# One of seven block products of a Strassen-type output projection is built from seven smaller ones

## The chip, the cores and the metric

The kernel runs on one core of one Trainium2 chip. The metric is the time of one execution on the device in microseconds (us). The profile is one execution, recorded by the hardware profiler: its times count from the first instruction, and its engines are called PE (TensorE, matrix products), PEld (its weight loads), DVE (VectorE), ACT (ScalarE), POOL (GpSimd) and SP (SyncE, which here only issues transfers).

## What is computed

One layer of a transformer trunk on 512 tokens of width 2048, all in 32-bit floats: a normalisation, attention over a sliding window of 128 tokens with 32 query heads, an output projection, a gated embedding, and a last normalisation.

```python
def reference(x, p, ...):
    hn = rmsnorm(x, norm_g)
    x = x + swa_mixer(hn, ...)              # ends with (out * silu(gate)) @ w_out
    emb = p @ ple_proj
    g = sigmoid(rmsnorm(x, ple_norm) @ ple_gate)
    x = x + emb * g
    return rmsnorm(x, final_g)
```

The change is within `(out * silu(gate)) @ w_out`: a 512 x 2048 matrix (the gated attention output, transposed in `gates`) times a 2048 x 2048 weight matrix, added to `x`.

## The kernel before

**Precision.** TensorE multiplies rounded 32-bit numbers (`F32R`). To keep the full precision, every operand is split into a high part (a cast on ACT) and a low part (the difference, on DVE), and `mm3` (lines 123 to 128) makes each product of three matmuls: high by high, high by low, low by high. A matmul takes a 128 x 128 stationary block and 128 x 512 moving columns.

**Stages.** First keys, values and the first queries; then a long stage in which attention runs beside the rest of the input projections (64 blocks of work in a loop, line 828); then the output projection (lines 967 to 1000); then the gate of the embedding with `ple_gate`, built the same way as the output projection (lines 1101 on); then the last rows. TensorE's and SP's instructions keep the order of the program. From line 870 to the second product of the gate, DVE, ACT and POOL are ordered by a planner, which puts an operation where it reckons the engine free and its inputs there.

**Seven products instead of eight.** For the output projection both matrices are cut into 2 x 2 blocks: the gated output into a11, a12, a21, a22 (1024 rows of the contraction or 256 tokens each way), the weights into four blocks of 1024 x 1024. Seven block products of sums of blocks give the result. They are numbered, and run in the order

```python
ORDER_OUT, ORDER_PLE = (1, 7, 2, 6, 5, 3, 4), (2, 7, 1, 6, 5, 3, 4)
```

Each product runs as two units (p, jj), one for each half of the block's 1024 columns (`unit`, line 903). A unit has four pieces m = 0 to 3. A piece is 128 x 1024 numbers of weights (512 KB): two chunks of 128 rows by 512 columns. With two blocks of 128 tokens, two chunks and three passes a piece gives 12 matmuls, a unit 48, a product 96. Products 6, 5 and 3 go on summing in the PSUM banks in which product 1 left its result (`chain`); the others take fresh banks. After a unit, `add_y` (line 950) adds or subtracts its two 128 x 512 results to `x1`, on DVE, from a list `later` of which some are put out after each piece. Results of product 1 are held back (`held`, `waiting`) until their place in `x1` has been loaded. When a 128 x 512 tile of `x1` is complete, `squares` sums its squares on ACT.

**Weight sums.** Products 7, 5 and 6 need sums of two weight blocks. They are made in DRAM while attention runs: `sum_weights` (line 640) copies one block to a scratch tile (issued on SP) and some steps later adds the other onto it by an adding transfer (issued on POOL), a step or two after each of the 64 blocks. `SUM_STEPS` counts them. Products 1, 2 and 3 take plain blocks of `w_out`. Product 4's piece is not loaded by itself: product 6's pieces lie in eight buffers of their own (`grown`, kind "seed"), and once a piece has been split, POOL adds product 4's block onto it there (kind "grow").

**Pieces.** The class `Pieces` (line 647) is the queue for the weight pieces. `get(i)` first looks ahead: it issues loads up to piece i + 3 (i + 4 in the gate stage, which has a fourth buffer, `fourth`), seeds up to i + 6, and splits pieces up to i + 2. A load waits until the piece that had its buffer has been split. There are three buffers for high parts and three for low parts (`whi`, `wlo`), so the cast of piece i + 3 waits until TensorE has finished piece i.

**Forms.** The token side is prepared by `Forms.steps` (line 755): for each product a sum of blocks on DVE where it needs one (in place, in `gates`), then high and low parts, in eight buffers, one product ahead.

Of the kernel before, what the change touches and what calls it, by code (L numbers as in the profile page):

```python
# [55 lines left out]
def trunk_kernel(ctx: ExitStack, tc: tile.TileContext, a: dict):  # L56
# [558 lines left out]

    def blk(t):
        return slice(t * P, (t + 1) * P)
# [3 lines left out]
    ORDER_OUT, ORDER_PLE = (1, 7, 2, 6, 5, 3, 4), (2, 7, 1, 6, 5, 3, 4)  # L621
# [9 lines left out]
    for nm, p in SUMS:  # L631
# [15 lines left out]
    class Pieces:  # L647
# [9 lines left out]
        def _prepare(self, i):  # L657
# [35 lines left out]
        def ahead(self, i):  # L693

            last = len(self.specs) - 9
            for n in range(max(i, 0), min(i + 6, last) + 1):
                kind = self.specs[n][0]
                if n not in self.base and n >= self.done and kind != "grow" and (kind == "seed" or n <= i + (4 if i >= at_ple[ORDER_PLE[0], 0] else 3)):
# [19 lines left out]
    def add_stage(nm, order):  # L718
# [7 lines left out]
        for p in order:  # L726
            for jj in range(2):
# [4 lines left out]
                at[p, jj] = len(B.specs)  # L732
                for m in range(4):
                    if (nm, p) in SUMS:
# [5 lines left out]
                    B.add(kind, src, (nm, jj, m) if p in growing else None)  # L740
                if p != 4:
# [4 lines left out]
    at_ple = add_stage("ple_gate", ORDER_PLE)  # L746

    class Forms:
# [154 lines left out]
    def unit(p, jj, at, forms, todo):  # L903
# [4 lines left out]
        for m in range(4):  # L908
            bh, bl = B.get(at[p, jj] + m)
# [6 lines left out]
            todo()  # L916
        return ps
# [31 lines left out]

    def add_y(p, jj, tb, ps):  # L950
        c11, c12, c21, c22 = ((2 * v + jj, 2 * u + tb) for u in range(2) for v in range(2))
        whither = {
            1: [(c11, -1)], 2: [(c11, 1)], 7: [(c22, 1), (c21, -1)], 6: [(c21, -1)], 5: [(c22, 1)], 3: [(c12, 1)],
            4: [(c21, 1)],
        }[p]
        for (j, t), sign in whither:
            xt = x1[j][:, t, :]
            if sign > 0:
                nc.vector.tensor_add(xt, ps, xt)
            else:  # L960
                nc.vector.tensor_sub(xt, xt, ps)
            if p in (2, 5, 3, 4):
                squares(t, j)
# [4 lines left out]
    waiting = {(7, 0): (1, 0), (2, 0): (1, 1)}  # L968
    held = {}
    for n, p in enumerate(ORDER_OUT):  # L970
        nxt = out_forms.steps(ORDER_OUT[n + 1]) if n < 6 else iter(())
        for jj in range(2):
            later.extend(held.pop(waiting.get((p, jj)), ()))
            calls = iter(range(4))

# [12 lines left out]
            ps = unit(p, jj, at_out, out_forms, todo)  # L988
# [99 lines left out]
    spare = late.tile([P, 2 * WE], F32R, name="spare")  # L1088
# [12 lines left out]
    for n, p in enumerate(ORDER_PLE[:-1]):  # L1101
# [8 lines left out]
        for jj in range(2):  # L1110
# [18 lines left out]
            if p in (1, 5, 3):  # L1129
                w = B.get(at_ple[p, jj] + 4)  # L1130
# [14 lines left out]
    def block(jj, tb, tag, e_tag, c=slice(0, 512)):  # L1145

        ps = bank(f"last{jj}_{tb}_{c.start}", tag)
        for k in range(8):
            fh, fl = f[k // 2]
            bh, bl = B.made[at_ple[4, jj] + k // 2]  # L1150
# [155 lines left out]
```

## Time and profile before

| | us |
|---|---|
| median of 3 runs | 797.12 |
| lowest and highest | 797.02, 797.53 |
| profiled execution, whole | 797.26 |
| its span, first to last instruction | 795.3 |

The mean granted clock of TensorE in the profiled execution was 0.996 of full speed. The span shares and the views of the trace stand in the prediction. To read them: a row of the timeline has the start, the duration, the engine, the line of the kernel and what is written from what, and in square brackets how long the engine stood idle before it and what ended that. A row of the stage view has, for each engine, busy microseconds and the count of instructions, then TensorE's granted clock, the busy share of the 16 DMA engines (overlapping records can bring it a little over 1) and GB/s. In the DMA view, `q1 hardware_dynamic` are the transfers that SP issues and `q0 software_dynamic` those that POOL issues, with packets, MB and the share of 16 engines; an issue's row ends with the microseconds until it has landed. A matmul's end is modelled: matmuls overlap, so their spacing and not their duration says what they take.

### The profile page before, as it was taken

How to read it: one execution, taken by the hardware profiler on the slowest of the kernel's cores; microseconds unless marked ns; L12 is line 12 of the kernel's file. 1: busy time of each engine (PE TensorE's matmuls, PEld its weight loads, DVE VectorE, ACT ScalarE, POOL GpSimd, SP SyncE). 2: the span in 40 equal slices, each digit the busy share in tenths (PEclk: the TensorE clock that was granted, in tenths of full speed). 3: DMA queues.
4: the chain of work that ended last, by engine and by line, in shares of the span. 5: the costliest groups of instructions: out<-in, count | busy, mean ns of one | idle time of the engine just before them, and what ended most of it. 6: DMA issues, size and time to landing. Idle time of an engine off the chain costs nothing.

```text
span 795.3 us, 10980 instructions
## 1 busy us (share of the span) xinstructions
PE 785.0 (99%) x3758; PEld 657.6 (83%) x3758; DVE 587.3 (74%) x1026; ACT 500.6 (63%) x1057; POOL 116.2 (15%) x238
## 2 busy tenths in 40 slices
PE   9999999999999999999999999999999999999995
PEld 8888888888888888888888888888888888888885
DVE  4547697877878597777768898766646757988896
ACT  6643576666767576666757655555568656656765
POOL 0021213131212213121212100030000020200000
PEclk9999999999999999999999999999999999999998
DMA  9983489697869968787875479997603996787633
GB/s 348 271 218 110 117 259 242 172 254 183 226 168 255 206 198 230 192 238 158 247 170 146 119 264 328 352 261 239 205 30 132 373 211 194 159 227 218 180 106 106
DMA packets 42919, 165.28 MB, mean 208 GB/s; under 512 B 6048, under 2 KB 7072, under 8 KB 39024
## 3 DMA queue, kind: packets, MB, share of 16 engines
q1 hardware_dynamic: 35456, 129.67, 48.5%
q0 software_dynamic: 7408, 34.93, 23.9%
q8 instruction: 29, 0.48, 0.2%
q14 instruction: 26, 0.21, 0.1%
HBM read 157.70 MB, written 46.19 MB: 256 GB/s over the span
## 4 chain that ended last, share of the span: by engine, by line
PE 98%; DMA 0%; DVE 0%; ACT 0%; issue 0%; ACTq 0%; DVEq 0%
PE gps L126 7%; PE gps L128 7%; PE gps L127 7%; PE qps L126 7%; PE qps L128 7%; PE qps L127 7%; PE o L126 6%; PE o L128 6%; PE o L127 6%; PE g L126 5%; PE g L127 5%; PE g L128 5%; PE s L462 2%; PE o L557 2%; PE vps L279 2%; PE pt L515 2%
## 5 line engine op out<-in xcount | busy, mean ns | idle before, releaser
L680 DVE TENSOR_TENSOR blo<-braw,bhi 128x1024 fp32r<-128x1024 f32 x80 | 97.8, 1222 | 39.7 <-ACT bhi L679 39.5
L679 ACT CAST bhi<-braw 128x1024 fp32r<-128x1024 f32 x80 | 84.2, 1052 | 65.6 <-PE o L128 19.8
L126 PE MATMUL gps<-xh,whi 128*128 128x512 f32 x256 | 99.9, 390 | 0.1
L128 PE MATMUL gps<-xh,wlo 128*128 128x512 f32 x256 | 99.9, 390 | 0.0
L127 PE MATMUL gps<-xl,whi 128*128 128x512 f32 x256 | 99.8, 390 | 0.0
L126 PE MATMUL o<-bhi,fho 128*128 128x512 f32 x224 | 87.7, 392 | 0.0
L126 PE MATMUL qps<-xh,whi 128*128 128x512 f32 x224 | 87.7, 391 | 0.0
L128 PE MATMUL qps<-xh,wlo 128*128 128x512 f32 x224 | 87.4, 390 | 0.0
L127 PE MATMUL qps<-xl,whi 128*128 128x512 f32 x224 | 87.3, 390 | 0.0
L128 PE MATMUL o<-bhi,flo 128*128 128x512 f32 x224 | 87.2, 389 | 0.0
L127 PE MATMUL o<-blo,fho 128*128 128x512 f32 x224 | 87.2, 389 | 0.0
L110 DVE TENSOR_TENSOR wlo<-wraw,whi 128x1024 fp32r<-128x1024 f32 x60 | 73.8, 1231 | 2.7 <-ACT whi L109 2.4
L126 PE MATMUL g<-bhi,fhg 128*128 128x512 f32 x192 | 75.1, 391 | 0.0
L128 PE MATMUL g<-bhi,flg 128*128 128x512 f32 x192 | 74.8, 389 | 0.0
L127 PE MATMUL g<-blo,fhg 128*128 128x512 f32 x192 | 74.7, 389 | 0.0
L531 POOL TENSOR_SCALAR_AFFINE_SELECT own<-r 64x512 fp32r<-64x512 f32 (+1 forms) x48 | 32.5, 677 | 255.8 <-DVE r L521 255.8
L520 ACT CAST r<-pt 128x256 fp32r<-128x256 f32 x64 | 23.8, 371 | 71.5 <-PE pt L515 71.1
L521 DVE TENSOR_TENSOR r<-pt,r 128x256 fp32r<-128x256 f32 x64 | 27.1, 424 | 55.5 <-ACT r L520 54.8
L109 ACT CAST whi<-wraw 128x1024 fp32r<-128x1024 f32 x60 | 62.4, 1041 | 5.3 <-issue 3.9
L680 DVE TENSOR_TENSOR blo<-grown,bhi 128x1024 fp32r<-128x1024 f32 x32 | 39.1, 1224 | 23.5 <-ACT bhi L679 23.4
L128 PEld LDWEIGHTS gps<-xh,wlo 128*128 128x128 f32 x256 | 48.0, 188 | 10.1
L126 PEld LDWEIGHTS gps<-xh,whi 128*128 128x128 f32 x256 | 48.1, 188 | 9.4 <-PE vps L279 0.5
(207 smaller groups left out, 1736.5 us busy)
## 6 DMA issues: line engine op xcount, KB each, us to landing
wraw<-in_w_gate_in SPq DMA_DIRECT2D x32, 512.0 KB, 5.7
wraw<-in_w_q SPq DMA_DIRECT2D x28, 512.0 KB, 5.0
w_out<-in_w_out POOLq DMA_DIRECT2D x24, 512.0 KB, 7.1
braw<-in_w_out SPq DMA_DIRECT2D x24, 512.0 KB, 4.0
braw<-in_ple_gate SPq DMA_DIRECT2D x24, 512.0 KB, 4.2
xw<-in_first SPq DMA_DIRECT2D x14, 640.5 KB, 6.5
w_out<-in_w_out SPq DMA_DIRECT2D x16, 512.0 KB, 5.8
ple_gate<-in_ple_gate SPq DMA_DIRECT2D x16, 512.0 KB, 6.6
```

Source lines behind the costliest of these rows:

```text
L109: nc.scalar.copy(hi, raw)
L110: nc.vector.tensor_sub(lo, raw, hi.bitcast(F32))
L126: nc.tensor.matmul(ps, sh, mh, start=first, stop=False, skip_group_check=more)
L127: nc.tensor.matmul(ps, sh, ml, start=False, stop=False, skip_group_check=more)
L128: nc.tensor.matmul(ps, sl, mh, start=False, stop=last, skip_group_check=more)
L279: nc.tensor.matmul(v_ps[t], h[:, c], both[:, :, 256:512], start=f, stop=e, skip_group_check=True)
L462: nc.tensor.matmul(s_ps[:, u, : 2 * n], st, key[:, :, first : first + n], start=True, stop=True)
L520: nc.scalar.copy(rh, src)
L521: nc.vector.tensor_sub(rl, src, rh.bitcast(F32))
L531: nc.gpsimd.affine_select(out=flat(own), in_=flat(r).bitcast(F32), pattern=[[0, 8], [sign, HB]], compare_op=ALU.is_ge, fill=0.0, base=-HB ...
L679: nc.scalar.copy(hi, raw)
L680: nc.vector.tensor_sub(lo, raw, hi.bitcast(F32))
```

## The change

Product 2 (a12 by one plain weight block of 1024 x 1024, added to the first quadrant of the result) is no longer run as a product of its own. Its two factors and its result are cut into 2 x 2 blocks again, 512 rows of the contraction by 128 tokens and 512 x 512 weights, and seven small products by the same scheme give it. A small product has two pieces of 128 x 1024 weights, each for one block of 128 tokens: 6 matmuls a piece. The pieces of the small products are placed behind pieces of the large ones (`SMALL`): two small pieces in each of the units (6,0), (6,1) and (3,0), four in (5,0) and (5,1).

What goes with it: small products 7, 5, 6 and 4 take sums of weights, two tiles each, which `sum_weights` makes beside the others (48 copies and 48 adding transfers instead of 40, in the same 64 blocks). Small forms are made on ACT and DVE from halves of `gates[2]` and `gates[3]`, with their sums in a buffer that the gate stage uses later (`spare`) and their parts in buffers that it uses later (`partial`). Product 3's form is now written over a11, so that a12 stays whole. Small 1, 6, 5 and 3 sum on in one bank. Each small result is added to (or subtracted from) one tile of `x1`, small 7's to two; a count `missing` says when a tile is complete. Product 1's second held results are released at (6,0). The fourth load buffer, and looking ahead to i + 4, start with product 6 instead of with the gate stage.

```diff
-    ORDER_OUT, ORDER_PLE = (1, 7, 2, 6, 5, 3, 4), (2, 7, 1, 6, 5, 3, 4)
+    ORDER_OUT, ORDER_PLE = (1, 7, 6, 5, 3, 4), (2, 7, 1, 6, 5, 3, 4)
+
+    SMALL = {
+        (6, 0): {1: 1, 3: 1}, (6, 1): {1: 7, 3: 7}, (5, 0): {0: 6, 1: 6, 2: 2, 3: 2},
+        (5, 1): {0: 4, 1: 4, 2: 5, 3: 5}, (3, 0): {1: 3, 3: 3},
+    }
...
-    for nm, p in SUMS:
+
+    def small_block(r, c, m):
+
+        return block("w_out", 2, 1, c - 1, 2 * (r - 1) + m)
+
+    for (nm, p), small in zip(SUMS, (7, 5, 6, 4, None)):
+        for m in range(2 if small else 0):
+            t = summed["small", small, m] = tc.dram_tile([P, WE], F32, name=f"small_{small}_{m}")
+            copies.append((t, {
+                7: small_block(1, 2, m), 5: small_block(1, 1, m), 6: summed.get(("small", 7, m)),
+                4: summed.get(("small", 6, m)),
+            }[small]))
+            adds.append((t, small_block(*{7: (2, 2), 5: (1, 2), 6: (1, 1), 4: (2, 1)}[small], m)))
...
-                    if rooms and i >= at_ple[ORDER_PLE[0], 0] and self.raws % 4 == 0:
+                    if rooms and i >= fourth_from and self.raws % 4 == 0:
...
+                    q = SMALL.get((p, jj), {}).get(m) if nm == "w_out" else None
+                    if q is not None:
+                        v = at.setdefault(("small", q), [])
+                        src = summed.get(("small", q, len(v)))
+                        if src is None:
+                            src = small_block(*{1: (1, 1), 2: (2, 1), 3: (2, 2)}[q], len(v))
+                        v.append(len(B.specs))
+                        B.add("one", src)
...
+    fourth_from = at_out[6, 0][0]
...
-                        5: (a21, (a21, a22)), 3: (a12, (a12, a11)), 4: (a22, None),
+                        5: (a21, (a21, a22)), 3: (a11, (a12, a11)), 4: (a22, None),
...
             some_later(4 - m)
             todo()
+            between(m)
...
+    def add_to_x(j, t, sign, ps):
+        xt = x1[j][:, t, :]
+        if sign > 0:
+            nc.vector.tensor_add(xt, ps, xt)
+        else:
+            nc.vector.tensor_sub(xt, xt, ps)
+        missing[j, t] -= 1
+        if not missing[j, t]:
+            squares(t, j)
...
+    def small_form(q):
+        a11, a12, a21, a22 = halves[0][:, 0], halves[1][:, 0], halves[0][:, 1], halves[1][:, 1]
+        src, sub = {
+            1: (a11, None), 2: (a12, None), 4: (a22, None), 7: (sigma, (a21, a11)), 6: (sigma, (a22, sigma)),
+            3: (sigma, (a12, sigma)), 5: (tau, (a21, a22)),
+        }[q]
...
+    small_made = {(7, 1): (1,), (6, 0): (7,), (6, 1): (6, 2), (5, 0): (4, 5), (5, 1): (3,)}
...
+    def small(q):
+
+        chained = q in (1, 6, 5, 3)
+        n = small_done[q] = small_done.get(q, -1) + 1
+        if n == 0:
+            if q == 1 or not chained:
+                small_ps[q] = bank(f"small{q}", "t" if chained else "o")
+            if chained:
+                small_ps[q] = small_ps[1]
+        bh, bl = B.get(at_out["small", q][n])
+        fh, fl = small_forms[q]
+        for kk in range(2):
+            k = 2 * n + kk
+            mm3(small_ps[q], fh[:, k], fl[:, k], bh[kk], bl[kk], k == 0 and q not in (6, 5, 3), k == 3, q in (6, 5, 3))
+        if n == 1:
+
+            to = {
+                1: [(0, 0, -1)], 2: [(0, 0, 1)], 7: [(1, 1, 1), (0, 1, -1)], 6: [(0, 1, -1)], 5: [(1, 1, 1)],
+                3: [(1, 0, 1)], 4: [(0, 1, 1)],
+            }[q]
+            later[:0] = [partial_of(add_to_x, *v, small_ps[q]) for v in to]
...
-    waiting = {(7, 0): (1, 0), (2, 0): (1, 1)}
+    waiting = {(7, 0): (1, 0), (6, 0): (1, 1)}
```

In the texts below, (6,0) is unit 0 of product 6, and "small 4" is the fourth small product.

More of the change, by code (lines that the diff above doesn't have):

```diff
@@ L901, in some_later, with unit @@
             later.pop(0)()
-    def unit(p, jj, at, forms, todo):
+    def unit(p, jj, at, forms, todo, between=lambda m: None):
         ps = banks(p, jj, forms.nm)
@@ L974, in trunk_kernel, with between @@
             calls = iter(range(4))
+            small_nxt = iter([step for q in small_made.get((p, jj), ()) for step in [small_form(q)]])
+            small_now = [next(small_nxt, None)]
+            def between(m):
+                if small_now[0] is not None and next(small_now[0], 0) == 0:
+                    small_now[0] = next(small_nxt, None)
+                q = SMALL.get((p, jj), {}).get(m)
+                if q is not None:
+                    small(q)
             def todo():
@@ L986, in todo @@
                         next(ple_first, None)
-            ps = unit(p, jj, at_out, out_forms, todo)
+            ps = unit(p, jj, at_out, out_forms, todo, between)
+            while small_now[0] is not None:
+                run(small_now[0])
+                small_now[0] = next(small_nxt, None)
             posts = [partial_of(add_y, p, jj, tb, ps[tb]) for tb in range(2)]
@@ L1084, in trunk_kernel @@
     moved = []
-    spare = late.tile([P, 2 * WE], F32R, name="spare")
+    spare = late.tile([P, 2 * WE], F32R, tag="spare", name="spare")
     rooms4 = {}
```

50 lines of the change are left out of this document (36 added, 14 removed).

## The prediction

> **What bounds the kernel now.** I read the page first (busy time, the chain that ended last), then cut the span by the stages of the code, then followed one product of the output projection engine by engine, and at last the DMA queues there.
>
> ```profile
> PE 785.0 (99%) x3758; PEld 657.6 (83%) x3758; DVE 587.3 (74%) x1026; ACT 500.6 (63%) x1057; POOL 116.2 (15%) x238
> PE 98%; DMA 0%; DVE 0%; ACT 0%; issue 0%; ACTq 0%; DVEq 0%
> ```
>
> TensorE is busy for 99% of the span and makes 98% of the chain that ended last: whatever takes matmuls away is worth its full time, as long as TensorE still never waits. The stage in question, from the timeline (two matmuls, twelve apart) and from the view of the tile `o`:
>
> ```profile
> L126 PE MATMUL o<-bhi,fho x224: 389/389/476, 451.8 to 608.9; 128*128 128x512 f32 x112
> ...
> 500.81 0.39 PE L126 MATMUL o<-bhi,fho 128*128 128x512 f32 x1
> ...
> 503.53 0.39 PE L126 MATMUL o<-bhi,fho 128*128 128x512 f32 x1
> ```
>
> A matmul's record says 0.39 us, but they overlap: twelve of them (one large piece: 2 chunks, 2 token blocks, 3 passes) take 503.53 - 500.81 = 2.72 us, 0.227 us each. Eight pieces are one product, 21.8 us. Cut at the product boundaries that follow from 451.8 (products 7, 2, 6, 5):
>
> ```profile
> core 0: us, PE busy (x) PEld busy (x) DVE busy (x) ACT busy (x) POOL busy (x), PEclk, DMA share, GB/s
> 473.60:495.40 21.80, 21.80 (x98) 18.05 (x97) 17.91 (x21) 10.75 (x13) 0.00 (x0) 1.00 0.95 347
> 495.40:517.20 21.80, 21.80 (x98) 18.06 (x97) 16.60 (x20) 11.79 (x17) 0.89 (x1) 1.00 0.89 339
> 517.20:539.00 21.80, 21.80 (x98) 18.06 (x97) 14.83 (x18) 11.79 (x17) 6.00 (x7) 1.00 1.06 254
> 539.00:560.80 21.80, 21.80 (x98) 18.06 (x97) 14.83 (x17) 11.78 (x17) 0.00 (x0) 1.00 0.74 240
> ```
>
> TensorE has no gap, but the DMA engines are full too: 0.95, 0.89, 1.06 of 16 engines through products 7, 2 and 6. So there is a second resource at its limit just where the change works. How close it comes, on ACT and DVE at the start of product 5:
>
> ```profile
> 544.45 1.05 ACT L679 CAST bhi<-braw 128x1024 fp32r<-128x1024 f32 x1 [4.01 <-DMA braw<-w_out]
> 545.53 1.22 DVE L680 TENSOR_TENSOR blo<-braw,bhi 128x1024 fp32r<-128x1024 f32 x1 [3.63 <-ACT bhi L679]
> ```
>
> ACT stood 4.01 us for a piece to land; cast and subtraction end at 546.75, 2.30 us after the landing. It is the fourth piece of product 5, due at 539.0 + 3 x 2.72 = 547.2. In hand: 0.4 us. Before the change this stage already comes within half a microsecond of stalling on a load.
>
> **What goes and what comes on TensorE.** Product 2 has 96 matmuls of 128x512. In its place come seven small products of 4 chunks x 3 passes = 12 matmuls of the same shape, 84 in all, the shape and the alternation of operands unchanged. 12 x 0.227 = **-2.7 us** if nothing waits. That is all there is to win. The change does what it says: the count follows from the loops.
>
> **What comes on ACT and DVE.** Pieces go from 8 (twelve matmuls each) to 14 (six each, 1.36 us), each still one cast and one subtraction. They alternate with large ones from product 6 on, never two in a row. Seven small forms and their sums, and eight small additions instead of four, are DVE work as well.
>
> ```profile
> L680 DVE TENSOR_TENSOR blo<-braw,bhi 128x1024 fp32r<-128x1024 f32 x80 | 97.8, 1222 | 39.7 <-ACT bhi L679 39.5
> ...
> 559.51 1.23 DVE L680 TENSOR_TENSOR blo<-braw,bhi 128x1024 fp32r<-128x1024 f32 x1 [0.26 <-ACT bhi L679]
> 560.65 1.28 DVE L959 TENSOR_TENSOR x1s<-o,x1s 128x512 f32<-128x512 f32 x2
> 561.85 0.68 DVE L785 TENSOR_TENSOR flo<-gate,fho 128x512 fp32r<-128x512 f32 x1
> ```
>
> Start to start a subtraction holds DVE for 1.14 us (559.51 to 560.65), an addition or form step of 512 columns for 0.60 (two in 560.65 to 561.85). Unit (5,0) of the changed kernel, 4 large and 4 small pieces, lasts 4 x 2.72 + 4 x 1.36 = 16.3 us. In it DVE has 8 splits (9.1), for product 3 two subtractions of 1024 and two forms (3.5), for small 4 and 5 two forms and one sum (1.8), five additions (3.0): 17.4 us, 1.1 more than the unit. The planner places DVE's work as soon as its inputs are there, and (6,0) with (6,1) have 12 splits (13.7), 4 large forms (2.4), small 7, 6 and 2 (3.0) and 9 additions (5.4), 24.5 of 27.2 us. So DVE fits on the whole, with little left; I take 0 for it, up to 4 us if it doesn't fit (second rival).
>
> Waits added: unit (6,1) goes on summing in the banks of (1,1), whose held additions (DVE, 0.60 each) now run within (6,0) instead of within product 2. The last is put out at (6,0)'s fourth piece, with 2.72 + 1.36 = 4.1 us of TensorE ahead of its first use: 0; if late, all of TensorE's queue stands behind it for 0.6 to 1.2 us. A small product that sums on in small 1's bank waits for the addition before it in the same way, a large piece ahead. The squares of the first quadrant move on ACT from product 6's time to products 5 and 3, where ACT has 10 of 21.8 us free: 0.
>
> **What comes on the DMA queues, early.** Eight more copies (SP) and eight more adding transfers (POOL) of 512 KB run during attention, 48 instead of 40 each over the same 64 blocks.
>
> ```profile
> 105.00:450.00 345.00, 345.00 (x1706) 290.37 (x1705) 266.67 (x585) 232.54 (x636) 77.41 (x168) 1.00 0.78 205
> ```
>
> At the prices worked out below (1.38 and 2.54 us) that is 31 us more of DMA: from 0.78 x 345 = 269 to 300 of 345 us, 0.87. POOL holds 77 us of work there. Not full, and projection pieces are asked for some three pieces ahead, so 0; should a load be late, each costs about 1 us, which I leave to the range.
>
> **What comes on the DMA queues, in the projection.** This is the term that decides. The order of things in the kernel before, from SP's and POOL's timeline:
>
> ```profile
> 474.54 5.46 SPq L672 DMA_DIRECT2D braw<-w_out  x3
> ...
> 487.70 11.10 SPq L672 DMA_DIRECT2D braw<-in_w_out  x5
> 498.85 0.42 SPq L672 DMA_DIRECT2D grown<-w_out  x1
> 500.81 0.33 SPq L672 DMA_DIRECT2D braw<-in_w_out  x1
> 501.24 0.37 SPq L672 DMA_DIRECT2D grown<-w_out  x1
> 503.35 0.33 SPq L672 DMA_DIRECT2D braw<-in_w_out  x1
> 503.73 3.43 SPq L672 DMA_DIRECT2D grown<-w_out  x6
> 507.25 4.88 SPq L672 DMA_DIRECT2D braw<-w_out  x3
> 512.40 0.33 SPq L996 DMA_DIRECT2D fg<-in_final_g  x1
> 536.28 12.57 SPq L672 DMA_DIRECT2D braw<-w_out  x5
> ```
>
> ```profile
> 514.79 0.89 POOL L661 DMA_DIRECT2D grown<-in_w_out  x1 [64.81 <-DMA grown<-w_out]
> ...
> 533.83 0.86 POOL L661 DMA_DIRECT2D grown<-in_w_out  x1 [1.58 <-DVE blo L680]
> ```
>
> Eight pieces of product 6 are loaded ("grown"), and as soon as each is split POOL adds product 4's piece onto it: eight adding transfers. Their speed, and that of plain loads, from the DMA view over four windows (485:495, 505:515, 525:535, 534:538), and last an unqueued load (446:460):
>
> ```profile
> q1 hardware_dynamic: 1350, 3.67, 99.5%
> ...
> q1 hardware_dynamic: 1089, 3.97, 101.2%
> ...
> q0 software_dynamic: 567, 2.06, 104.2%
> ...
> q0 software_dynamic: 228, 0.84, 106.4%
> braw<-w_out SPq DMA_DIRECT2D x1, 512.0 KB, 8.1
> ...
> braw<-in_w_out SPq DMA_DIRECT2D x3, 512.0 KB, 3.2
> ```
>
> With all 16 engines busy, plain loads move 3.67 to 3.97 MB in 10 us: 1.43 to 1.32 us for 512 KB (0.524 MB), middle 1.38. Adding transfers move 2.06 MB in 10 us: 2.54 us each. A load by itself lands after 3.2, so about 1.9 beyond its own transfer. And the load issued at 536.28 landed 8.1 us later: between 534 and 538 no packet of its queue moved while the adding transfers, issued before, were served. So I reckon with one line, first come, first served. Test on before: from 498.5 (the last of the five at 487.70) to the load at 536.28 there are 16 units of 512 KB (1 + 8 grown + 2 + 3, fg twice), eight adding transfers, and the load: 17 x 1.38 + 8 x 2.54 = 43.8, plus 1.9: 544.2. ACT got it at 544.45. The ledger holds.
>
> The same for the changed kernel. Products 1 and 7 are as before, so 6 begins at 495.4. Take the third large piece of unit (5,0): ahead of it lie 10 large and 6 small pieces, 35.4 us, so it is due at 530.8 and must have landed 2.3 us earlier, at **528.5**. From 474.5 on, up to and with it, SP asks for product 7's last four pieces (4), two quarters of x (4 units), eight grown (8), small 1 and 7 (4), the first five pieces of (5,0) (5) and fg (2): 27 units. All eight adding transfers are ahead of it: the last grown piece is split at about 517, while this load must wait for a buffer until (5,0)'s first piece is split, 495.4 + 23.1 + 2.3 = 520.8. So 27 x 1.38 + 8 x 2.54 = 57.6, and 474.5 + 57.6 + 1.9 = **534.0**: 5.5 us late. With 1.32 us a unit 3.9 late, with 1.43 6.9. What product 2 gave before was time: 21.8 us of TensorE for 11 us of loads, in which the line drained; that cover is gone, and small pieces ask for 512 KB per 1.36 us. Behind (5,0) the need is 1.38 us of DMA per 2.04 us of TensorE and the adding transfers are through: no further wait.
>
> By the Trainium skill, "DMA: Bandwidth & Descriptors", section "Queues, rings and completion order", each DMA engine takes turns between the queues it has work for. The 534:538 row speaks against it (no turn for the load). By that rule the last four units (from 519) would run at half speed beside the adding transfers, 519 + 4 x 2.76 + 1.9 = 532, 3.5 us late, and the sum +0.8 instead of +2.8.
>
> **Sum.** -2.7 + 5.5 = +2.8 us. The profiled execution took 797.26 us (span 795.3), 0.14 over the median of 797.12; so 797.1 + 2.8 = **799.9**; own range 798.3 to 801.3.
>
> **The rivals.** *Loads are in time (faster).* If the line drains by 528.5, because SP's loads pass the adding transfers, nothing waits: 797.1 - 2.7 = 794.4. For it: nothing on TensorE waits today even at 1.06. Against: the 8.1 us. It decides at 7.7 us from issue (520.8) to landing; I reckon 13. Chance 0.15.
>
> *DVE becomes the bound (about no change).* Loads half hidden, but DVE's 1.1 us too much in (5,0), and in each of three other alternating units two additions ahead of a split (1.2 us; a small and a large piece leave 4.08 - 2.3 = 1.8): 1.1 to 4.7, net -1.6 to +2.0, about 797.3. For it: 17.4 against 16.3. Against: DVE is not on the chain today. Chance 0.17.
>
> *The clock falls (slower still).* After TensorE's last matmul, which ended at 786:
>
> ```profile
> 786.00:788.00 2.00, 0.11 (x1) 0.00 (x0) 1.87 (x7) 1.86 (x3) 0.00 (x0) 1.00 0.00 0
> 788.00:790.00 2.00, 0.00 (x0) 0.00 (x0) 1.73 (x6) 1.58 (x5) 0.00 (x0) 0.64 0.00 0
> 790.00:795.00 5.00, 0.00 (x0) 0.00 (x0) 0.20 (x1) 0.24 (x1) 0.00 (x0) 0.50 0.59 211
> ```
>
> A mean of 0.64 over 788 to 790 with 0.50 after it means that it fell at 788.6, 2.6 us after work ended. A stall of 5.5 us, taken at one piece or two neighbours, could do that in the middle; if it takes 2.6 us to return, 1.3 us more are lost and the wait may come in one piece: 801.2 to 802.5. The Trainium skill, "TensorE: Matmul & The Clock Gate", section "What's actually happening", gives windows of about 3.4 us for both ways, by which 1.7 us would be lost. Chance 0.20.
>
> **Numbers.** 0.2% of the time, 1.6 us, is about what a measurement of this kernel can tell from no change. Forecast 0.48, of which 0.05 is its lower end inside 0.2%; rivals 0.15, 0.17, 0.20. Faster 0.15, same 0.22, slower 0.63. The range 794.3 to 802.5 takes in all cases but the tails.
>
> **What would show it.** TensorE 12 matmuls fewer; a new idle time of some 5 us on TensorE near 525 to 537, ended by `blo`, ACT's casts before it waiting for `braw`; the DMA share at 1.0 from 475 to 533; braw loads then landing after 10 us and more. Wrong if TensorE has no gap there (loads in time), if the gaps are short, many, and ended by DVE without ACT waiting for DMA (DVE), or if idle time appears before 450 (the added sums).

## The result, and the profile after

| | kernel before | changed kernel |
|---|---|---|
| median, lowest to highest (6 runs each) | 797.35, 797.02 to 798.05 | 803.26, 800.79 to 804.34 |
| ratio, 95% interval | | 1.0067, 1.0049 to 1.0085 |
| profiled execution, its span | 797.26, 795.3 | 800.96, 799.2 |

The change makes the kernel slower by 5.9 us in the medians and 3.7 in the profiled executions. The forecast was +2.8, its range up to 802.5. The sign and the place of the loss came out; the size did not, and 803.26 lies above the range.

The page of the changed kernel (engines, then its chain):

```profile
PE 784.5 (98%) x3746; PEld 655.1 (82%) x3746; DVE 599.7 (75%) x1043; ACT 508.0 (64%) x1066; POOL 122.5 (15%) x246
PE 32%; DMA 5%; DVE 3%; issue 1%; ACT 1%; ACTq 0%; DVEq 0%
```

TensorE has the 12 matmuls fewer, but its chain, unbroken before, now runs over transfers and DVE. Next the tile `o` (lowest, median and highest duration in ns, first and last start), what TensorE waited for in the output projection (us in all, times, longest), and TensorE's timeline at these waits:

```profile
L126 PE MATMUL o<-bhi,fho x192: 387/389/503, 451.8 to 613.2; 128*128 128x512 f32 x192
```

```profile
PE o L127 <- DVE blo L699: 2.7, 3, 1.2
PE o L126 <- ACT bhi L698: 2.0, 2, 1.1
```

```profile
492.61 0.39 PE L126 MATMUL o<-bhi,fho 128*128 128x512 f32 x1
494.20 0.50 PE L127 MATMUL o<-blo,fho 128*128 128x512 f32 x1 [1.20 <-DVE blo L699]
...
529.57 0.50 PE L126 MATMUL o<-bhi,fho 128*128 128x512 f32 x1 [1.06 <-ACT bhi L698]
530.83 0.50 PE L127 MATMUL o<-blo,fho 128*128 128x512 f32 x1 [0.76 <-DVE blo L699]
...
534.21 0.50 PE L127 MATMUL small<-blo,small_forms 128*128 128x512 f32 x1 [0.32 <-DVE blo L699]
...
536.59 0.49 PE L126 MATMUL o<-bhi,fho 128*128 128x512 f32 x1 [0.93 <-ACT bhi L698]
537.85 0.50 PE L127 MATMUL o<-blo,fho 128*128 128x512 f32 x1 [0.77 <-DVE blo L699]
```

The stage starts at 451.8 as before and ends 4.3 us later. The brackets count idle time from a matmul's modelled end; what a gap costs is the distance between two starts less the usual 0.227: 494.20 - 492.61 - 0.227 = 1.36. Called gaps below are such distances over 0.3 us, from TensorE's timeline. Here they are 1.36 at 494 and 4.9 us in five between 529 and 538; slow restarts (0.11 each) bring it to about 6.9. Less the 2.7 won that is +4.2; the span grew by 3.9.

The stages, cut at the changed kernel's boundaries where product 6 begins:

```profile
core 0: us, PE busy (x) PEld busy (x) DVE busy (x) ACT busy (x) POOL busy (x), PEclk, DMA share, GB/s
473.60:495.40 21.80, 20.60 (x91) 16.77 (x90) 21.49 (x27) 11.14 (x13) 0.00 (x0) 1.00 1.00 384
495.40:509.00 13.60, 13.60 (x61) 11.26 (x61) 10.72 (x13) 5.80 (x6) 3.48 (x4) 1.00 1.05 317
509.00:522.70 13.70, 13.70 (x63) 11.33 (x62) 10.43 (x12) 8.05 (x10) 3.40 (x4) 1.00 1.05 274
522.70:540.00 17.30, 13.46 (x53) 9.40 (x52) 11.17 (x14) 7.90 (x9) 0.00 (x0) 1.00 0.95 315
```

The DMA engines are full from 473 to 535, and 522.7 to 540 is where TensorE stands. The late load itself, the third large piece of (5,0): its issue on SP, the DMA view of 523:524 with the microseconds to its landing, and ACT's timeline:

```profile
523.20 0.32 SPq L691 DMA_DIRECT2D braw<-w_out  x1
```

```profile
braw<-w_out SPq DMA_DIRECT2D x1, 512.0 KB, 12.2
```

```profile
528.47 1.04 ACT L698 CAST bhi<-braw 128x1024 fp32r<-128x1024 f32 x1 [2.70 <-DMA braw<-w_out]
...
531.85 1.05 ACT L698 CAST bhi<-braw 128x1024 fp32r<-128x1024 f32 x1 [1.29 <-DMA braw<-small]
...
535.49 1.04 ACT L698 CAST bhi<-braw 128x1024 fp32r<-128x1024 f32 x1 [2.60 <-DMA braw<-w_out]
```

Issued at 523.20, it landed at 535.4. Each time ACT stood for a load before its cast. At the large pieces TensorE then stood twice: for the high part, and 1.26 us later (529.57 to 530.83, 536.59 to 537.85) for the low one.

### The profile page after: what moved, and what is told of

It reads as the page before. It is cut to its first block, busy times and chain, and to the rows that moved or that the text cites. A ratio compares the mean times of both kernels' runs of the same rounds, so it can differ in the third digit from the quotient of the medians.

```text
span 799.2 us, 11043 instructions
## 1 busy us (share of the span) xinstructions
PE 784.5 (98%) x3746; PEld 655.1 (82%) x3746; DVE 599.7 (75%) x1043; ACT 508.0 (64%) x1066; POOL 122.5 (15%) x246
## 5 line engine op out<-in xcount | busy, mean ns | idle before, releaser
L699 DVE TENSOR_TENSOR blo<-braw,bhi 128x1024 fp32r<-128x1024 f32 x86 | 104.8, 1220 | 37.5 <-ACT bhi L698 37.1
L698 ACT CAST bhi<-braw 128x1024 fp32r<-128x1024 f32 x86 | 90.5, 1052 | 62.6 <-PE g L128 18.8
L127 PE MATMUL o<-blo,fho 128*128 128x512 f32 x192 | 75.1, 391 | 2.7 <-DVE blo L699 2.7
L126 PE MATMUL o<-bhi,fho 128*128 128x512 f32 x192 | 75.5, 393 | 2.0 <-ACT bhi L698 2.0
L128 PE MATMUL o<-bhi,flo 128*128 128x512 f32 x192 | 74.9, 390 | 0.0
```

Source lines behind the costliest of these rows:

```text
L126: nc.tensor.matmul(ps, sh, mh, start=first, stop=False, skip_group_check=more)
L127: nc.tensor.matmul(ps, sh, ml, start=False, stop=False, skip_group_check=more)
L128: nc.tensor.matmul(ps, sl, mh, start=False, stop=last, skip_group_check=more)
L698: nc.scalar.copy(hi, raw)
L699: nc.vector.tensor_sub(lo, raw, hi.bitcast(F32))
```

## The experiments

The theory: **the loads**. The transfers of the output projection do not fit between product 7 and product 5, and pieces land late. Rivals: **DVE** is too slow for the many splits; the **clock** falls at stalls and makes most of the loss; and once the loads were confirmed, that any moved transfer only moves the gaps. In the table, "us" is the median, gaps are sums by place in the profiled run, and a half clock is a stretch of matmuls 0.427 apart in it.

| kernel | us (runs) | ratio to before, 95% | gaps before 500 | 500 to 545 | after 545 | half clock |
|---|---|---|---|---|---|---|
| changed, again | 801.05 (5) | 1.0035 to 1.0060 | 1.6 | 4.7 | 0 | none |
| no_grow | 796.08 (10) | 0.9973 to 0.9991 | 2.2 | 0 | 0 | at 496 |
| order_only | 799.56 (8) | 1.0016 to 1.0036 | 1.6 | 1.4 | 0 | none |
| x_fg | 799.02 (11) | 1.0009 to 1.0027 | 3.5 | 1.0 | 0 | none |
| fg_only | 799.93 (8) | 1.0014 to 1.0034 | 1.9 | 2.5 | 0 | at 532 |
| seed_early | 804.73 (4) | 1.0075 to 1.0101 | 6.2 | 2.1 | 0 | none |
| seed_early_fg | 803.96 (6) | 1.0062 to 1.0087 | 4.6 | 2.6 | 0 | at 490 |
| no_fourth | 804.34 (1) | one run | 1.8 | 5.4 | 0.9 | at 537 |
| late_grow | 800.14 (6) | 1.0019 to 1.0043 | 1.6 | 0 | 3.6 | none |
| late_grow_fg5 | 799.00 (11) | 1.0009 to 1.0028 | 0.4 | 0 | 3.4 | none |
| spread | 794.27 (5) | 0.9951 to 0.9978 | 0 | 0 | 0 | none |
| spread_only | 796.83 (11) | 0.9980 to 0.9998 | 1.5 | 0.7 | 0 | none |

**The changed kernel again**, five executions, nothing edited.

> The changed kernel once more, unaltered, for the spread of its times. Theory 1 (loads in one line with the adding transfers): every run has the same stalls of 6.5 to 7 us on TensorE between 490 and 540, and runs near 801 us. Theory 2 (the clock falls besides): the runs above 803 us have a mean granted clock of 0.990 to 0.993 instead of 0.996; 0.004 of 800 us is 3.2 us, as much as they are longer. If the runs above 803 show 0.996, the spread is in the length of the stalls and not in the clock.

801.05, 800.81 to 802.21: +3.6 over before measured beside it (797.43), where the first six executions gave +5.9. Gaps at the same places as in the first profile. The first six went up to 804.34, these five did not; more on that under the clock.

**no_grow**: the eight adding transfers of product 4's pieces in the output projection are left out (so product 4 multiplies with product 6's pieces).

```diff
-                nc.gpsimd.dma_start(t, src, accum_op=ALU.add)
+                if key[0] != "w_out":
+                    nc.gpsimd.dma_start(t, src, accum_op=ALU.add)
```

> The changed kernel without the output projection's eight adding transfers (product 4 takes product 6's weights alone; that part of the computation is left out). Theory 1: 8 x 2.54 = 20 us of transfers are gone from the line, the loads of unit (5,0) land within 5 us, TensorE has no gap between 520 and 540; left is the gap of 1.4 us at 494, which lies ahead of the first adding transfer: 797.3 - 2.7 + 1.4 = 796.0, or 794.6 without that gap. Rival (DVE is the bound in unit (5,0)): DVE's work is unchanged, so gaps of 1 to 5 us stay between 522 and 540, and the time stays above 798.

796.08, as reckoned (796.0), and no gap behind 500: all 4.7 us of the late gaps hang on these transfers. DVE's work on the pieces is the same here, so DVE was not what stopped unit (5,0). What stayed in the profiled execution (797.73, the longest of ten) is one gap of 2.2 us at 495, and behind it a fall of the clock. The stage view across that gap, and the same view further on:

```profile
494.00:496.00 2.00, 1.00 (x4) 0.86 (x5) 2.00 (x3) 0.96 (x2) 0.00 (x0) 0.99 1.03 420
496.00:499.00 3.00, 3.00 (x8) 2.34 (x7) 2.19 (x4) 0.12 (x1) 0.00 (x0) 0.50 1.03 419
...
505.00:510.00 5.00, 5.00 (x24) 4.14 (x23) 2.45 (x2) 3.03 (x3) 0.00 (x0) 1.00 0.25 92
...
520.00:525.00 5.00, 5.00 (x24) 4.14 (x23) 3.98 (x4) 2.48 (x3) 0.00 (x0) 1.00 0.33 84
...
585.00:590.00 5.00, 5.00 (x28) 4.18 (x27) 2.31 (x2) 3.57 (x9) 0.00 (x0) 1.00 0.00 0
```

In 496 to 499 the granted clock is 0.50 and 8 matmuls fit where 13 would: about 1.5 us lost. And the last column but one (the DMA share) says where there would be room: 505 to 525, and 585 on.

**order_only**: the kernel before, with product 6 ahead of product 2 and no small products.

```diff
-    ORDER_OUT, ORDER_PLE = (1, 7, 2, 6, 5, 3, 4), (2, 7, 1, 6, 5, 3, 4)
+    ORDER_OUT, ORDER_PLE = (1, 7, 6, 2, 5, 3, 4), (2, 7, 1, 6, 5, 3, 4)
...
-    waiting = {(7, 0): (1, 0), (2, 0): (1, 1)}
+    waiting = {(7, 0): (1, 0), (6, 0): (1, 1)}
```

> The kernel before, with product 2 moved behind product 6 (order 1, 7, 6, 2, 5, 3, 4), and no small products: what the missing 22 us ahead of product 6 do alone, with DVE's load as before. Theory 1: the last large piece of unit (2,0) is due at 495.4 + 11 x 2.72 = 525.3 and must land by 523.0; up to it the line holds 4 + 4 + 8 + 4 + 2 = 22 units and eight adding transfers, 474.5 + 22 x 1.38 + 8 x 2.54 + 1.9 = 527.1, so 4 us late: 797.3 + 4 = 801, within 800 to 803, with the gap near 527. Rival (the small pieces with their 512 KB in 1.36 us, or DVE, make the stall): no gap, 797.3, the same as before.

799.56: +2.1 us over before (797.43, measured beside it) without a single small piece. Both forecasts missed: the theory had one gap of 4 us near 527, the rival none. It waits for low parts, 1.6 us at 495 and 1.4 near 531 and 535:

```profile
PE o L127 <- DVE blo L680: 2.5, 3, 1.4
```

ACT's casts before the two later ones had stood for loads (2.80 us at 528.83, 2.74 at 532.61). So part of the loss, 3.0 of 6.3 us by the gaps of the profiled executions, comes with product 2 no longer standing ahead of product 6's eight loads and eight adding transfers; that the small pieces add the rest is a difference of two kernels. The early gap is here in full: it needs no small piece.

**Taking other transfers out of the way.** `x_fg` asks for all quarters of x within product 1 and for `final_g` after product 3; `fg_only` moves `final_g` alone.

```diff
-    x_at = {(1, 1, 1): 0, (7, 0, 0): 2, (7, 0, 3): 1, (7, 1, 1): 3}
+    x_at = {(1, 0, 1): 0, (1, 0, 3): 2, (1, 1, 1): 1, (1, 1, 3): 3}
...
-        if p == 6:
+        if p == 3:
             nc.sync.dma_start(fg, ...)
```

> The changed kernel with two loads moved: the four quarters of x (1 MB each) are asked for in units (1,0) and (1,1), where the DMA share was 0.57 to 0.60, instead of from (1,1) to (7,1); and final_g (1 MB) behind product 3 instead of behind product 6. Theory 1: from 474.5 to the third large piece of (5,0) the line is 4 + 2 = 6 units shorter, 8.3 us, more than the 7 us that were lost: no gap on TensorE, 797.3 - 2.7 = 794.6, within 794 to 796. Rival (DVE): unchanged work on DVE, the gaps stay, 800 or more. Rival (the clock): no gap, so nothing that could bring it down, 0.996 in every run.

> The changed kernel with final_g alone moved behind product 3. Theory 1 (one line of transfers): 2 units, 2.8 us, leave the line ahead of the third large piece of (5,0). The changed kernel's gaps between 520 and 540 came to 5.0 us in its last profile and shrink to 2 to 2.5; the one of 1.6 us at 494, ahead of final_g, stays: 801.1 - 2.8 = 798.3, within 797.8 to 799. Rival (the gaps at 530 and 536 come from DVE's order): they stay, 801.

Neither came out as the theory had it: 799.02 and 799.93. With both moved the late gaps fell from 4.7 to 1.0 us, but the early ones rose from 1.6 to 3.5. The two longest of these are the order of DVE, not late loads: before the gap at 473.84 the high part was there at 471.92, the subtraction began at 472.56 behind a sum and a form step, and ACT had not stood for a load. `fg_only` took 2.2 us from the late gaps, and its early gap stayed (1.9). In its profiled execution the clock fell behind the last of the late ones:

```profile
532.00:535.00 3.00, 3.00 (x8) 2.32 (x8) 1.68 (x3) 1.93 (x2) 0.00 (x0) 0.50 0.86 335
```

That cost some 1.5 us there (800.28). It does not explain the median: two executions of `fg_only` took 800.13 and 800.50 at a mean clock of 0.998.

**Asking for product 6's pieces earlier**: one a piece, up to 16 pieces ahead from piece 3 on (`seed_early`), and the same with `final_g` after product 3 (`seed_early_fg`).

```diff
+            far = 3 <= i < at_out[6, 0][0]
-            for n in range(max(i, 0), min(i + 6, last) + 1):
+            for n in range(max(i, 0), min(i + (16 if far else 6), last) + 1):
...
+                    if n > i + 6:
+                        if not far:
+                            continue
+                        far = False
```

> The changed kernel with product 6's eight loads asked for one per piece from product 1's fourth piece on, up to 16 pieces ahead instead of 6, so in the time from 457 to 490 in which the line was idle for some 40%; DVE's and ACT's work is untouched. Theory 1: as much as the line was idle there (about 8 us) is gained ahead of (5,0); the gaps between 520 and 540 are 1 us or less, the one at 494 stays or grows to 2.5 (x's quarters wait behind the early loads): 801.1 - 4.5 = 796.6, within 795.5 to 798. Rival (DVE): gaps between 520 and 540 as before, 801. It also tells whether it was x's move or the shorter line that made x_fg's new gaps between 467 and 487: here x's additions keep their place.

> Both moves, product 6's loads early and final_g late. Theory 1: no gap after 500, one of 1 to 2.5 us at 494: 797.4 - 2.7 + 1.1 to 2.5 = 795.8 to 797.2, so at best about 1.5 us faster than the kernel before. Rival (DVE): 799 or more.

Worse than the change run again: 804.73 and 803.96, where under 798 was expected. The wait at 489.9 alone is 2.8 us. TensorE's waits, then ACT and DVE ahead of it, in `seed_early`:

```profile
PE o L127 <- DVE blo L699: 5.6, 5, 2.8
...
483.72 1.05 ACT L698 CAST bhi<-braw 128x1024 fp32r<-128x1024 f32 x1 [3.96 <-DMA braw<-w_out]
...
486.27 0.69 DVE L993 TENSOR_TENSOR x1s<-o,x1s 128x512 f32<-128x512 f32 x1 [1.60 <-PE o L128]
...
488.67 2.35 DVE L699 TENSOR_TENSOR blo<-braw,bhi 128x1024 fp32r<-128x1024 f32 x2
```

The load was late (ACT stood 3.96 us for it), and these loads do go ahead of product 7's own pieces, which are wanted sooner. But the high part was there at 484.77, when DVE was idle; DVE then waited for TensorE and did four additions of a unit that had just ended before the subtraction at 488.67. With the subtraction at once the low part would have been there at about 486.0, before the matmul due at 487.0. So the 3.0 us of this gap are DVE's order, which the planner had set. And the room that the expectation counted on was not there: it took the line from 457 to 490 for 40% idle, but the DMA share is 1.00 from 473.6 on (stage view above).

**no_fourth**: the fourth load buffer, and the look ahead to i + 4, only from the gate stage, as before the change.

```diff
-    fourth_from = at_out[6, 0][0]
+    fourth_from = at_ple[ORDER_PLE[0], 0][0]
```

> The changed kernel without the fourth load buffer in the output projection (loads 3 pieces ahead there, as before the change). Theory 1: what counts is the sum of transfers ahead, not the buffers; loads are asked for some 2 to 4 us later, but land when the line has drained: gaps between 520 and 540 of 5 to 7 us in all, 801 to 803. Rival (too few buffers is what delays the loads): gaps grow by 2 us and more in every unit with small pieces, (5,1) and (3,0) too: above 805.

Gaps of 8.1 us in all instead of 6.3, and 804.34 in its one run, as long as the longest of the first six of the changed kernel; the clock fell in it too. By the gaps the deeper look ahead helps TensorE here rather than hurts; as a time, one run leaves it open.

**Pushing the adding transfers back.** `late_grow` puts each out up to 26 pieces behind the one it adds to instead of 6, with two one-column operations on POOL that need the newest low part and add zero, so that it cannot start sooner; `late_grow_fg5` also moves `final_g` behind product 3 and asks for product 6's pieces 5 ahead instead of 6.

```diff
+                if key[0] == "w_out":
+                    lo = self.lo.bitcast(F32)
+                    nc.gpsimd.tensor_sub(nil, lo[:, :1], lo[:, :1])
+                    nc.gpsimd.tensor_add(t[:, :1], t[:, :1], nil)
                 nc.gpsimd.dma_start(t, src, accum_op=ALU.add)
...
-                    self.due.append((i + 6, n))
+                    self.due.append((min(i + 26, 51) if key[0] == "w_out" else i + 6, n))
...
-            for n in range(max(i, 0), min(i + 6, last) + 1):
+            for n in range(max(i, 0), min(i + (5 if i < fourth_from else 6), last) + 1):
```

The last pair of lines is in `late_grow_fg5` alone.

> The changed kernel with the eight adding transfers of the output projection (product 4's pieces onto product 6's) held back: each is put out 26 pieces behind the piece it adds to, instead of 6, and POOL first does two operations on one column that need the newest split, so that the transfer can't start sooner. Nothing is left out. Line of loads (the adding transfers take their 8 x 2.5 = 20 us out of the line between 500 and 535, and there is room for them behind 545, where the DMA share was 0.83 to 0.48): the gaps at 529 to 538 go as they went when the adding transfers were left out, the one at 494 to 495 of 1.4 to 2.2 us stays, so -2.7 + 2 = 796 to 797.5. Rival, the same work only makes the same gaps elsewhere (as with the loads of product 6 asked for earlier): 3 to 5 us of gaps come back between 545 and 590, 799.5 to 801.5. Rival, DVE is the bound once loads are in time: gaps ended by DVE with no cast waiting for DMA, near 525 to 540.

> As late_grow, and with it final_g's transfer after product 3 and product 6's loads asked for up to 5 pieces ahead instead of 6. Nothing is left out. Line of loads: two more units gone from the line ahead of product 5 and the loads of product 6 a little less early ahead of product 7's pieces, so the gap near 494 shrinks to about 1 us or goes: 794.6 to 796.0, under the kernel before. Rival, gaps come back behind 545: 798 to 800. Rival, the early gap is DVE's own order of work and not the line: it stays at 1.5 to 2 us, 796 to 797.5, as for late_grow.

800.14 and 799.00, both missed: the gaps of 500 to 545 went, and 3.6 and 3.4 us came back behind 570, as the rival had it. The stage view of `late_grow_fg5`:

```profile
560.00:575.00 15.00, 13.81 (x60) 10.78 (x59) 7.92 (x8) 5.84 (x10) 5.06 (x13) 1.00 1.05 284
575.00:590.00 15.00, 13.45 (x62) 10.52 (x61) 8.46 (x8) 10.65 (x20) 4.38 (x7) 1.00 1.04 318
```

The DMA share that was 0.76 and 0.48 there in the changed kernel is now 1.05 and 1.04: the eight transfers were moved past the free stretch of 505 to 525 into the gate stage's first loads. The early gap is 1.6 in `late_grow` and 0.4 in `late_grow_fg5`.

**spread**: as `late_grow_fg5`, with the transfers at the places that `no_grow` showed free, and `final_g` after product 4. `spread_only` has the places alone.

Against the changed kernel, beside the two POOL operations and the look ahead of 5 shown above:

```diff
+    GROW_AT = {16: 19, 17: 20, 19: 21, 20: 22, 22: 23, 23: 34, 25: 43, 26: 53}
...
-                    self.due.append((i + 6, n))
+                    self.due.append((GROW_AT[i] if key[0] == "w_out" else i + 6, n))
...
-        if p == 6:
+        if p == 4:
             nc.sync.dma_start(fg, ...)
```

> As late_grow_fg5, but the adding transfers are put where the line stood idle when they were left out (DMA share 0.25 to 0.33 from 505 to 525, 0.8 from 525 to 580, 0 from 585 to 605): five of them from about 504 on, one near 539, one near 555, one near 577, and final_g's transfer after product 4, where the share is 0. Nothing is left out. Line of loads (the whole transfer work fits, only its place was wrong): 5 x 2.54 = 12.7 us into some 14 us that were free, no gap over 1 us behind 500, the early one 0.5: -2.7 + 0.5 to 1 = 795.0 to 796.0, faster than the kernel before. Rival, moved transfers only move the gaps: 2 to 4 us of gaps somewhere between 515 and 580, 797.5 to 800.

> The changed kernel with the adding transfers at the places of the kernel spread (794.27), but final_g's transfer after product 6 and product 6's loads up to 6 pieces ahead, as the change has them. Nothing is left out. Line of loads: the places of the adding transfers are worth nearly all of the late gaps; the early one at 494 (1.4 to 2.2 us) stays, and final_g's two units at 522 meet the last of the five transfers: up to 2.8 us late for one piece of product 5, of which its buffers cover about half. 796.0 to 798.0. If the places alone are worth it all, 794.5 to 795.5; if they are worth nothing without final_g's move, gaps of 3 to 5 us at 527 to 540 and 799 to 801.

`spread` takes 794.27 us against 797.30 measured beside it: ratio 0.9965, 0.9951 to 0.9978, a little better than the 795.0 to 796.0 expected. No wait of TensorE is left in the stage. Its stage view and its tile `o`:

```profile
473.60:495.40 21.80, 21.80 (x97) 18.02 (x96) 21.80 (x28) 11.15 (x13) 0.00 (x0) 1.00 0.97 360
495.40:509.00 13.60, 13.60 (x61) 11.26 (x60) 11.79 (x15) 6.58 (x7) 1.66 (x5) 1.00 1.03 396
509.00:522.70 13.70, 13.70 (x62) 11.33 (x61) 10.80 (x13) 8.21 (x11) 4.63 (x10) 1.00 1.03 210
522.70:540.00 17.30, 17.30 (x78) 14.35 (x77) 15.22 (x18) 10.45 (x12) 1.24 (x3) 1.00 0.88 287
```

```profile
L126 PE MATMUL o<-bhi,fho x192: 388/390/477, 452.3 to 606.6; 128*128 128x512 f32 x192
```

The same transfers, all of them, now fit: the share is 1.03 from 495 to 522 and TensorE is at 21.80 of 21.80, 13.60 of 13.60, and so on. This is the version that clearly beats both kernels. `spread_only`, 796.83 and within what was expected, has a gap of 1.5 at 494 and one of 0.7 at 534: the places are worth 4.2 of the 6.8 us between the changed kernel run again (801.05) and `spread`, the other two edits 2.6 (4.5 and 2.1, each against the kernel before measured beside it). Of these two, the look ahead of 5 is what takes the early gap: `final_g` is issued only at 520, and moved alone (`fg_only`) it left the gap at 1.9. How they share the rest was not run.

## Why the prediction was right and wrong

**The step that failed.** "Products 1 and 7 are as before" put nothing on product 7. In its place TensorE stood 1.36 us there, because its last piece landed later and DVE had 3.6 us more to do (21.49 us busy instead of 17.91). With it the gaps give +4.2; the profiled execution, 800.96, and the repeat, 801.05, lie at the upper end of my own range. The rest up to 803.26, some 2 us, is in no profile. It is likely in part the clock, for which I had asked a stall of some 5.5 us and which fell at gaps of less than half of that in other kernels; the cause of this part stays open.

**The gain: right.** 3758 - 3746 is 12 matmuls. `spread`, where nothing waits, is 3.0 us under before; 2.7 was reckoned.

**The added sums during attention: right, 0.** The stage starts at 451.8 in both.

**The late piece of unit (5,0): right in place, near in size.** Due to land at 528.5, reckoned at 534.0, landed at 535.4, as my dear price of 1.43 us a unit would have it (535.3); 5.5 us of stall reckoned there, 4.9 measured in the profile (4.7 in the second). The early gap and the late ones hang together: the piece landed 6.9 us behind 528.5, and 6.9 is what TensorE lost in all. If the transfers ahead alone set the landing, the gap at 494 only took its 1.4 us from the later ones, and the 1.4 that the sum lacks can be booked on either; no run takes away the first gap alone. The issue came at 523.2 instead of 520.8, which should not have mattered, as the DMA engines were full ahead of it. The row named as the one to look for, idle time near 525 to 537 with ACT's casts waiting for `braw`, is there; the DMA share is at 1.0 to 535.

**One line, first come first served: wrong, without harm to the sum.** From the window 534:538 of before, in which only the adding transfers' queue moved, I concluded that a load waits until those issued ahead are through. The DMA view of the changed kernel in 516:520, then of before in 540:542:

```profile
q0 software_dynamic: 155, 0.57, 70.8%
q1 hardware_dynamic: 154, 0.54, 36.4%
```

```profile
q0 software_dynamic: 69, 0.25, 63.6%
q1 hardware_dynamic: 76, 0.31, 41.5%
```

155 packets to 154, and 150 to 151 in 524:528: the two queues take turns. In before, too, the load issued at 536.28 got its turns from 540 on; I had looked only at its first 1.7 us. This is the rule of the Trainium skill, "DMA: Bandwidth & Descriptors", section "Queues, rings and completion order" (each DMA engine takes turns between the queues it has work for), which I had held to be refuted; the traces bear it out. The sum survived because the ledger adds all work up: where the adding transfers are through before the piece lands (here between 530 and 532), both orders give the same landing. My estimate by the rule, 532, came out too early because it let only four units share with them, while in 516 to 528 all of SP's loads did, at 0.55 MB in 4 us.

**"Products 1 and 7 are as before": wrong; the term that was missing.** A gap of 1.4 us at 494 in the first profile, 1.5 to 2.2 in the others that ask for x and for product 6's pieces as the change does. Product 6's loads now follow product 7's in SP's order, and so go out between product 7's pieces and the last quarters of x. SP of the changed kernel, and the cast that ACT made for the last piece of product 7, at which TensorE stood; then that piece's cast and subtraction in before:

```profile
480.18 1.02 SPq L691 DMA_DIRECT2D grown<-w_out  x1
481.25 0.43 SPq L951 DMA_DIRECT2D x1s<-in_x  x1
...
490.45 1.05 ACT L698 CAST bhi<-braw 128x1024 fp32r<-128x1024 f32 x1
```

```profile
488.79 1.05 ACT L679 CAST bhi<-braw 128x1024 fp32r<-128x1024 f32 x1 [0.98 <-DMA braw<-w_out]
...
489.87 1.23 DVE L680 TENSOR_TENSOR blo<-braw,bhi 128x1024 fp32r<-128x1024 f32 x1 [0.39 <-ACT bhi L679]
```

The load had been issued at 483.25 and landed 7.1 us later, at 490.35; in before it was issued at 482.00 and landed at 488.7. The cast came 1.66 us later than in before. There the subtraction followed it at once, here it did not. DVE of the changed kernel at the same time:

```profile
487.06 1.21 DVE L699 TENSOR_TENSOR blo<-braw,bhi 128x1024 fp32r<-128x1024 f32 x1
...
489.40 1.22 DVE L801 TENSOR_TENSOR gate<-gate,gate 128x1024 f32<-128x1024 f32 x1
490.53 1.27 DVE L990 TENSOR_TENSOR x1s<-x1s,o 128x512 f32<-128x512 f32 x2
491.73 0.68 DVE L814 TENSOR_TENSOR flo<-gate,fho 128x512 fp32r<-128x512 f32 x1
492.33 0.68 DVE L1015 TENSOR_TENSOR small_sums<-gate,small_sums 128x512 f32<-128x512 f32 x1
492.93 1.22 DVE L699 TENSOR_TENSOR blo<-braw,bhi 128x1024 fp32r<-128x1024 f32 x1
```

Between two splits, 487.06 and 492.93, DVE did 4.7 us of additions and forms without a pause. The high part for the second was there at 491.5 (490.45 + 1.05); the subtraction stood 1.4 us behind work that the planner had put ahead of it, and TensorE lost 1.4 us. With the subtraction at once the low part would have been there at about 492.7, just in time for the matmul due at 492.84 (492.61 + 0.227). So the later load used up the time in hand, and DVE's order made the gap. I had counted DVE for units (6,0) to (5,0), and not for product 7.

Was DVE the bound there? Not by the amount of its work: in `spread` it is busy 21.80 of 21.80 and nothing waits. There the planner ordered it otherwise:

```profile
490.41 1.06 ACT L704 CAST bhi<-braw 128x1024 fp32r<-128x1024 f32 x1 [2.14 <-PE o L127]
...
491.87 1.22 DVE L705 TENSOR_TENSOR blo<-braw,bhi 128x1024 fp32r<-128x1024 f32 x1
...
494.14 1.29 DVE L821 TENSOR_TENSOR flo<-gate,fho 128x512 fp32r<-128x512 f32 x2
```

The matmul was due at 493.34 here, 0.5 us later, so against it the cast came 0.5 us sooner than in the changed kernel; but the subtraction came 1.6 us sooner, because the second form step, ahead of it there (491.73), and the small sum (492.33) now lie behind it. In `late_grow_fg5`, with the same order, the cast came at 491.06, later than in the changed kernel, and the gap is 0.4. So asking for product 6's pieces one less ahead took the gap away, as far as these rows show, mostly through the order that the planner then chose, and only in part through an earlier load.

**The clock: the rival's mechanism, at a smaller stall than I asked of it.** I let it fall only at a stall of some 5.5 us. It fell at 2.2 (`no_grow`), at 1.1 and 1.0 with a few matmuls between (`fg_only`), at 1.9 and 1.0 (`no_fourth`), and not at 1.6 and 1.0 (the changed kernel again) nor at 3.0 in `seed_early`, though in `seed_early_fg` it fell at the same gap. Each fall is 3 to 3.4 us at half speed and costs some 1.5 us. The Trainium skill, "TensorE: Matmul & The Clock Gate", section "What's actually happening", has free-running windows of about 3.4 us, and a fall after an idle one. The length of the slow stretch, and that the same gap does it in one kernel and not in another, agree with such windows; that a wholly idle one is needed does not, since no gap reached 3.4 us. Whether a certain share of a window must be idle was not tested. In the first six executions of the changed kernel the granted clock was 0.996 and 0.995 at 800.96 and 800.79, and 0.990 to 0.992 at 803.51 to 804.34. At 1.5 us a fall, two or three falls would make these 3 us; the sixth, 803.02 at 0.996, does not fit. So the share of +5.9 that is clock may be about 2 of 6 us, and is only argued: the profiled execution shows none. Longer gaps are a rival that no run rules out: `late_grow_fg5` ranges from 796.89 to 800.87 at 0.996 to 0.998.

**The rivals.** Loads in time (794.4) became true once the transfers were placed where the line was free (794.27). DVE as the bound of unit (5,0) fell with `no_grow`; in product 7 it was DVE's order that TensorE waited for, a place that this rival did not name.

Altogether: -2.7, +4.9 (5.5 reckoned), +1.4 and 0.6 of restarts (both left out), and in some executions perhaps +1.5 for each fall (reckoned as a rival, for a longer stall). My own range ended at 801.3 because the bounds were put on one term, the price of a unit in the line, and none on the product that I had taken to be unchanged.

## What to carry to other kernels

Ask of every product that a change leaves "as it is" what is now issued ahead of its loads, and what now stands ahead of its operations on a full engine: an order moves more than the edited lines. Where an operation waits, see first whether its input was there; at 494 and 489.9 it was. When transfers are the bound, moving them can just pass the lateness on; leave the suspected transfers out once, read in the windows where the DMA share falls, and put them back there. A row that shows one queue served and another not says little if the second had nothing ready yet: look at the next microseconds too.

## What the runs showed of the hardware

- Two DMA queues with work moved as many packets each (155 to 154 in 4 us), and the adding transfers took nearly twice the time for the same bytes: 70.8% of the engines' share against 36.4% for 0.57 and 0.54 MB.
- In before, the load issued at 536.28 into busy DMA engines had moved 6 packets by 540, where an unqueued one lands in 3.2 us; after that it took its turns. Its queue in 538:540:

```profile
q1 hardware_dynamic: 6, 0.02, 3.2%
```

- TensorE's granted clock went to half behind gaps of 1.1 and 1.0 us and of 2.2 us, for 3 to 3.4 us, and the same gap of 3.0 us had a fall behind it in one kernel and none in another.
